# Splitting, merging and thinning the transfers of an RMS norm on one core

## The chip, the cores and the metric

The kernel runs on one NeuronCore of a Trainium2 chip. The metric is the device time in microseconds (us), as the median of several runs. Times of the kernel before and of the changed kernel are compared only between runs on the same chip, taken in turn, and all of them were at a granted clock of 1.0. DVE is the profile's name for the vector engine, ACT for ScalarE, POOL for GpSimd.

## The reference

```python
x: (16, 1024, 512) float32, gamma: (512,) float32
rms = np.sqrt(np.mean(x ** 2, axis=-1, keepdims=True) + 1e-5)
return (x / rms * gamma).astype(np.float32)
```

That is 16,384 rows of 512 floats: 33.5 MB in and 33.5 MB out, with little arithmetic on each element.

## The kernel before

The rows are cut into four tiles of 128 partitions x 32 rows (8.4 MB each), held in three buffers; tile 3 takes the buffer of tile 0. One sequencer issues every transfer, in program order.

```python
def load(t, slot, r0, r1):
    dma = nc.sync.dma_start(out=slots[slot][:, r0:r1], in_=xv[t][:, r0:r1])
    ...
def store(t, slot, r0, r1):
    dma = nc.sync.dma_start(out=ov[t][:, r0:r1], in_=slots[slot][:, r0:r1])
    ...
load(0, 0, 0, 8)
for c0, c1 in zip(pieces, pieces[1:]):          # gamma in five pieces
    nc.sync.dma_start(out=gamma_row[:, c0:c1], in_=gamma.unsqueeze(0)[:, c0:c1])
load(0, 0, 8, 16)
load(0, 0, 16, 32)
load(1, 1, 0, 32)
```

The rows of a partition lie next to each other in memory, so a transfer of n rows makes one packet of n x 2 KB for each partition, and on each of the 16 DMA engines it ends with a packet of 4 bytes for its semaphore. The compute goes in groups of up to 16 rows. ScalarE squares the rows of the next group and scales its share of the present one, DVE sums squares and multiplies by gamma, and GpSimd scales and multiplies the last `share` rows alone.

```python
groups = [                     # tile, first row, rows, pieces for the squares, GpSimd's share
    (0, 0, 7, (7,), 2), (0, 7, 9, (4, 5), 4), (0, 16, 16, (7, 5, 4), 7),
    (1, 0, 16, (7, 5, 4), 8), (1, 16, 16, (7, 5, 4), 8), (2, 0, 16, (7, 5, 4), 8),
    (2, 16, 16, (7, 5, 4), 7), (3, 0, 16, (7, 5, 4), 7), (3, 16, 16, (7, 5, 4), 3),
]
def transfers(t, g):           # issued after the group (t, g)
    if (t, g) == (0, 0):
        store(0, 0, 0, 1); load(2, 2, 0, 16)
        store(0, 0, 1, 2); load(2, 2, 16, 24)
        store(0, 0, 2, 3); load(2, 2, 24, 32)
    elif (t, g) == (0, 16):
        store(0, 0, 3, 16); store(0, 0, 16, 32)
        load(3, 0, 0, 16); load(3, 0, 16, 32)
    elif (t, g) == (1, 16): store(1, 1, 0, 32)
    elif (t, g) == (2, 0):  store(2, 2, 0, 16)
    elif (t, g) == (2, 16): store(2, 2, 16, 32)
    ...                        # tile 3 in two halves
```

(Lines are joined here to save space.)

## Time and profile before

| | before |
|---|---|
| time, median of three runs | 161.52 us (161.43 to 161.56) |
| span in the profile | 159.6 us |
| busy: DVE, ScalarE, GpSimd | 70%, 68%, 68% |
| DMA queue: data moved, share of 16 engines | 67.1 MB, 98.2% |
| last compute instruction ends | 142.2 us |
| last data packet ends | 158.4 us |

A profile like this is read from its end; the prediction below does it, with the lines. A line in the order of issues holds the start, the time that the issues took up to the end of the last, the queue (SPq is the sequencer of SyncE) and what it moved. A line of the stretches view holds the stretch, its length, busy time and count of PE, its weight loads, DVE, ScalarE and GpSimd, the clock, the DMA share, and GB/s.

### The profile page before, as it was taken

To read this page: it belongs to the slowest core of one execution; us is meant where nothing else is said; L and a number is where in the kernel's file an instruction comes from. 1 tells how busy PE (TensorE), PEld (TensorE's weight loads), DVE (VectorE), ACT (ScalarE), POOL (GpSimd) and SP (SyncE) were. 2 spreads that over 40 slices of the span, in tenths; PEclk is the share of its full clock that TensorE was granted. 3 is DMA by queue.
4 is the path that set the end of the run, shared out by engine and by line. 5 is a ranking of instruction groups with operands and counts; after the bars stand their busy time and mean duration, and the time that the engine had idled before them with its cause. 6 is when DMAs were issued, how large, how long until landed. Compare 5 with 4: busy or idle time off the path is not lost.

```text
span 159.6 us, 280 instructions
## 1 busy us (share of the span) xinstructions
PE 2.0 (1%) x2; PEld 0.5 (0%) x2; DVE 111.8 (70%) x43; ACT 108.5 (68%) x110; POOL 108.2 (68%) x24
## 2 busy tenths in 40 slices
PE   0050000000000000000000000000000000000000
PEld 0010000000000000000000000000000000000000
DVE  0027298998069899999999999999999809700000
ACT  3072999960499997989989989999995198000000
POOL 1000731981999309999999999999999999960000
DMA  5999999969799999999999999996999999999995
GB/s 199 419 435 485 435 394 526 526 263 526 329 394 396 454 415 419 427 452 444 476 394 402 509 402 394 526 526 263 526 394 394 394 501 419 394 452 468 394 419 238
DMA packets 2747, 67.12 MB, mean 421 GB/s; under 512 B 313, under 2 KB 314, under 8 KB 698
## 3 DMA queue, kind: packets, MB, share of 16 engines
q1 hardware_dynamic: 2746, 67.11, 98.2%
q14 instruction: 1, 0.01, 0.0%
HBM read 33.56 MB, written 33.55 MB: 421 GB/s over the span
## 4 chain that ended last, share of the span: by engine, by line
POOL 49%; DMA 26%; ACT 8%; DVE 3%; POOLq 2%; issue 0%
POOL slot L103 26%; DMA slot<-in_x_dram 26%; POOL slot L102 23%; ACT slot L111 3%; DVE slot L115 3%; ACT sq_psum L89 3%; POOLq L205 2%; ACT sq_sbuf L89 1%; DVE ss L96 0%; POOLq L102 0%
## 5 line engine op out<-in xcount | busy, mean ns | idle before, releaser
L102 POOL TENSOR_TENSOR slot<-slot,ss 128x3584 f32<-128x3584 f32 (+4 forms) x9 | 47.8, 5310 | 32.7 <-DVE ss L96 32.7
L90 DVE TENSOR_REDUCE ss<-sq_psum 128x7 f32<-128x3584 f32 (+1 forms) x16 | 49.1, 3066 | 20.1 <-ACT sq_psum L89 20.1
L103 POOL TENSOR_TENSOR slot<-slot,gamma_b 128x3584 f32<-128x3584 f32 (+4 forms) x9 | 60.2, 6692 | 0.7
L111 ACT ACTIVATE slot<-slot,ss 128x512 f32<-128x512 f32 x74 | 46.8, 707 | 4.7 <-DVE ss L96 4.7
L89 ACT ACTIVATE sq_psum<-slot 128x3584 f32<-128x3584 f32 (+1 forms) x16 | 40.2, 2510 | 12.4 <-DMA slot<-in_x_dram 11.0
L115 DVE TENSOR_TENSOR slot<-slot,gamma_psum 128x4608 f32<-128x4608 f32 (+4 forms) x10 | 40.8, 4093 | 4.9 <-ACT slot L111 4.9
L90 DVE TENSOR_REDUCE ss<-sq_sbuf 128x5 f32<-128x2560 f32 x8 | 22.4, 2805 | 0.0
L89 ACT ACTIVATE sq_sbuf<-slot 128x2560 f32<-128x2560 f32 x8 | 18.6, 2323 | 0.0
L95 ACT ACTIVATE ss<-ss,eps_t 128x16 f32<-128x16 f32 (+2 forms) x9 | 2.7, 303 | 4.2 <-DVE ss L90 4.2
L95 ACT ACT_TABLE_LOAD x1 | 1.3, 1283 | 4.0 <-DVE ss L90 4.0
L96 DVE RECIPROCAL ss<-ss 128x16 f32<-128x16 f32 (+2 forms) x9 | 2.1, 235 | 1.7 <-ACT ss L95 1.7
L65 PE MATMUL gamma_psum<-gamma_row,ones_col 1*128 1x512 f32 x2 | 2.0, 1118 | 8.7 <-DMA gamma_row<-in_gamma_dram 8.7
L89 ACT ACT_TABLE_LOAD x1 | 1.3, 1283 | 1.1 <-PEq L194 1.1
L160 ACT COPY gamma_b<-gamma_psum 128x512 f32<-128x512 f32 x1 | 0.6, 566 | 0.0
L65 PEld LDWEIGHTS gamma_psum<-gamma_row,ones_col 1*128 1x128 f32 x2 | 0.5, 308 | 8.7 <-issue 8.7
L63 POOL MEMSET ones_col<- 1x128 f32 x1 | 0.2, 194 | 0.3 <-POOLq L194 0.3
L194 POOL MEMSET const-float32-0.0<- 128x1 f32 x1 | 0.1, 98 | 0.2 <-issue 0.2
L194 POOL MEMSET const-bfloat16-1.0<- 128x1 bf16 x1 | 0.1, 101 | 0.0
L194 POOL MEMSET const-uint8-127<- 128x1 uint8 x1 | 0.1, 101 | 0.0
L194 POOL MEMSET const-float32-1.0<- 128x1 f32 x1 | 0.1, 98 | 0.0
L69 POOL MEMSET eps_t<- 128x1 f32 x1 | 0.1, 88 | 0.0
## 6 DMA issues: line engine op xcount, KB each, us to landing
out_dram<-slot SPq DMA_DIRECT2D x5, 4096.0 KB, 16.6
slot<-in_x_dram SPq DMA_DIRECT2D x4, 4096.0 KB, 19.3
slot<-in_x_dram SPq DMA_DIRECT2D x4, 2048.0 KB, 9.9
out_dram<-slot SPq DMA_DIRECT2D x1, 3328.0 KB, 32.4
out_dram<-slot SPq DMA_DIRECT2D x3, 256.0 KB
gamma_row<-in_gamma_dram SPq DMA_DIRECT2D x4, 0.4 KB
gamma_row<-in_gamma_dram SPq DMA_DIRECT2D x1, 0.5 KB
slot<-in_x_dram SPq DMA_DIRECT2D x1, 34.3
```

The source lines that it names most:

```text
L65: nc.tensor.matmul(gamma_psum[:, 0], ones_col, gamma_row, start=True, stop=True)
L89: nc.scalar.activation(out=sq[:, :m], in_=rows, func=AF.Square)
L90: nc.vector.tensor_reduce(out=ss[:, r : r + m, 0], in_=sq[:, :m], axis=mybir.AxisListType.X, op=OP.add)
L95: nc.scalar.activation(out=ss[:, :n, 0], in_=ss[:, :n, 0], func=AF.Sqrt, bias=eps_t, scale=1.0 / D)
L96: nc.vector.reciprocal(out=ss[:, :n, 0], in_=ss[:, :n, 0])
L102: nc.gpsimd.tensor_tensor(out=part, in0=part, in1=by_row, op=OP.mult)
L103: last = nc.gpsimd.tensor_tensor(out=part, in0=part, in1=gamma_b.to_broadcast([P, share, D]), op=OP.mult)
L111: nc.scalar.activation(out=x[:, g + r, :], in_=x[:, g + r, :], func=AF.Copy, scale=rstd[:, r])
L115: scaled = nc.vector.tensor_tensor(out=part, in0=part, in1=gamma_psum.to_broadcast([P, r1 - r0, D]), op=OP.mult)
L160: nc.scalar.copy(out=gamma_b[:, 0], in_=gamma_psum[:, 0])
L194: nc = _bacc.Bacc("TRN2", target_bir_lowering=False, num_devices=1)
L205: with _tile.TileContext(nc) as tc:
```

## The change

It rearranges transfers. Tile 1 comes in two halves, so that its first half can be squared 10 us sooner. Tile 2 is loaded and stored in one piece each. Of the three early single-row stores only the first stays. Gamma comes in one piece. GpSimd's shares are evened out, the square root's table is loaded at the start, and the last product of DVE is no longer split. GpSimd's shares and the last edit are given in words; `...` marks a cut.

```diff
-    for c0, c1 in zip(pieces, pieces[1:]):
-        nc.sync.dma_start(out=gamma_row[:, c0:c1], in_=gamma.unsqueeze(0)[:, c0:c1])
+    nc.sync.dma_start(out=gamma_row, in_=gamma.unsqueeze(0))
     load(0, 0, 8, 16)
     load(0, 0, 16, 32)
-    load(1, 1, 0, 32)
+    load(1, 1, 0, 16)
+    load(1, 1, 16, 32)
...
+    table = const.tile([P, 1], fp32)
+    nc.scalar.activation(out=table, in_=eps_t, func=AF.Sqrt)
...           (GpSimd's shares: 2, 4, 7, 8, 8, 8, 7, 7, 3 become 3, 5, 7, 7, 7, 7, 7, 7, 3)
             store(0, 0, 0, 1)
-            load(2, 2, 0, 16)
-            store(0, 0, 1, 2)
-            load(2, 2, 16, 24)
-            store(0, 0, 2, 3)
-            load(2, 2, 24, 32)
+            load(2, 2, 0, 32)
         elif (t, g) == (0, 16):
-            store(0, 0, 3, 16)
+            store(0, 0, 1, 16)
...
-        elif (t, g) == (2, 0):
-            store(2, 2, 0, 16)
         elif (t, g) == (2, 16):
-            store(2, 2, 16, 32)
+            store(2, 2, 0, 32)
...           (one times_gamma per group, the last group's too)
```

More of the change, by code (lines that the diff above doesn't have):

```diff
@@ L52 @@
     gamma_row = const.tile([1, D], fp32)
-    pieces = (0, 128, 224, 320, 416, D)
     load(0, 0, 0, 8)
-    for c0, c1 in zip(pieces, pieces[1:]):
-        nc.sync.dma_start(out=gamma_row[:, c0:c1], in_=gamma.unsqueeze(0)[:, c0:c1])
+    nc.sync.dma_start(out=gamma_row, in_=gamma.unsqueeze(0))
     load(0, 0, 8, 16)
     load(0, 0, 16, 32)
-    load(1, 1, 0, 32)
+    load(1, 1, 0, 16)
+    load(1, 1, 16, 32)
     ones_col = const.tile([1, P], fp32)
@@ L69 @@
     nc.gpsimd.memset(eps_t, eps)
+    table = const.tile([P, 1], fp32)
+    nc.scalar.activation(out=table, in_=eps_t, func=AF.Sqrt)
     groups = [
-        (0, 0, 7, (7,), 2),
-        (0, 7, 9, (4, 5), 4),
+        (0, 0, 7, (7,), 3),
+        (0, 7, 9, (4, 5), 5),
         (0, 16, 16, (7, 5, 4), 7),
-        (1, 0, 16, (7, 5, 4), 8),
-        (1, 16, 16, (7, 5, 4), 8),
-        (2, 0, 16, (7, 5, 4), 8),
+        (1, 0, 16, (7, 5, 4), 7),
+        (1, 16, 16, (7, 5, 4), 7),
+        (2, 0, 16, (7, 5, 4), 7),
         (2, 16, 16, (7, 5, 4), 7),
@@ L170 @@
         scale(rstd, t, g, 0, half)
-        if not ahead:
-            times_gamma(t, g, 0, half)
         for piece in todo[2:]:
@@ L175 @@
         scale(rstd, t, g, half, mine)
-        times_gamma(t, g, 0 if ahead else half, mine)
+        times_gamma(t, g, 0, mine)
         transfers(t, g)
```

## The prediction

> **What bounds the kernel now.** I read the page first, then the chain that ended last, then the DMA queue's own waits, then the stretches table, and last the order of the issues. The page has this on engines and queue:
>
> ```profile
> PE 2.0 (1%) x2; PEld 0.5 (0%) x2; DVE 111.8 (70%) x43; ACT 108.5 (68%) x110; POOL 108.2 (68%) x24
> ...
> DMA  5999999969799999999999999996999999999995
> ...
> DMA packets 2747, 67.12 MB, mean 421 GB/s; under 512 B 313, under 2 KB 314, under 8 KB 698
> ...
> q1 hardware_dynamic: 2746, 67.11, 98.2%
> ```
>
> No compute engine is busy above 70% of the span, while packets of the one DMA queue fill 98.2% of the time of 16 engines. A few slices show 6 or 7. I distrust those, because a packet of 64 KB is counted in the slice where it starts. The chain that ended last seems to contradict the DMA reading:
>
> ```profile
> POOL 49%; DMA 26%; ACT 8%; DVE 3%; POOLq 2%; issue 0%
> ```
>
> ```profile
> 128.16 7.79 POOL slot L103
> 135.96 2.70 POOL slot L102
> 138.66 0.04 issue
> 138.70 3.45 POOLq L205
> ```
>
> But that chain stops at 142.15 us of a span of 159.6. The 17 us after it hold no compute at all. What ends them is in the waits of the issuing sequencer (us in total, times, longest):
>
> ```profile
> SPq L49 <- DVE slot L115: 52.2, 7, 20.5
> SPq L49 <- POOL slot L103: 36.0, 5, 9.2
> SPq L45 <- DMA out_dram<-slot: 20.8, 2, 11.1
> ...
> SPq L205 <- DMA out_dram<-slot: 16.0, 2, 9.6
> ```
>
> The sequencer ends by waiting 16.0 us for the last two stores. So the end is a store's landing, not GpSimd. The long waits above it are waits before an issue; they matter only if the engines run dry meanwhile. The stretches table (the last two columns are DMA share and GB/s) says that they don't:
>
> ```profile
> 12.00:41.50 29.50, 0.00 (x0) 0.00 (x0) 22.93 (x11) 19.82 (x20) 14.56 (x5) 1.00 1.00 427
> 41.50:63.00 21.50, 0.00 (x0) 0.00 (x0) 16.92 (x6) 20.68 (x19) 14.54 (x3) 1.00 1.02 430
> ...
> 121.50:140.00 18.50, 0.00 (x0) 0.00 (x0) 12.59 (x5) 8.38 (x14) 18.34 (x5) 1.00 1.01 438
> ...
> 158.40:159.60 1.20, 0.00 (x0) 0.00 (x0) 0.00 (x0) 0.00 (x0) 0.00 (x0) 1.00 0.00 0
> ```
>
> The share is 1.0 in each of the first three, also where the compute waits for data, and in the last 1.2 us nothing moves. In the trace's packet records the first packet starts at 1.75 us and the last ends at 158.41 us, and in every 1 us bin between them 16 packets are in flight on average, to within one. The kernel is one unbroken stream of 156.7 us, plus 1.75 us ahead and 1.2 us behind. The reported time is 161.52 - 159.6 = 1.9 us more than the span. A change helps only by shortening the stream, and hurts only by making it longer or putting a hole in it.
>
> **What the Trainium skill says.** "DMA: Bandwidth & Descriptors", section "Where 436 GB/s comes from", gives 435.2 GB/s as the ceiling of the SBUF ports and about 358 as the HBM share of a core. The trace agrees with the first: 67.11 MB in 156.66 us are 428 GB/s. It does not show the 358 with this core alone. The same page, section "Anatomy of one DMA — SWDGE (gpsimd) path", says that DMA engines do not wait on semaphores; the issuing sequencer waits, and the engines drain their queues. The trace agrees: the sequencer waits tens of us and the stream has no hole. Its section "Bandwidth" (Measured) advises at least 1 MiB per DMA. That was measured on single transfers; the 256 KB row stores here queue behind other work, so I size their cost from the packets instead. "ScalarE: Activation LUTs", section "What ACT_TABLE_LOAD costs", has about 1283 ns for a table load; the two loads here took 1283 ns each.
>
> **The change part by part.** A 128-partition transfer gives each of 16 engines 8 packets, one per partition. Median packet times in the records are 0.084 us for 2 KB, 0.611 for 16 KB, 0.987 for 26 KB, 1.213 for 32 KB and 2.418 for 64 KB. A straight line fits all of them: 9 ns per packet plus bytes at 27.2 GB/s. A semaphore packet of 4 bytes took 9 ns too. The bytes don't change, so the stream changes by 9 ns for every packet per engine.
>
> Before: 9 loads of x and 10 stores, 19 x 8 = 152 data packets per engine (2,432 / 16 in the records), and 19 semaphore packets. After: 8 loads (three of tile 0, two of tile 1, one of tile 2, two of tile 3) and 7 stores (row 0 of tile 0, rows 1 to 15, rows 16 to 31, tile 1, tile 2, two halves of tile 3). That is 15 x 8 = 120 data packets and 15 semaphore packets.
>
> - Second tile in two halves: 8 more packets, +0.072 us.
> - Third tile loaded whole instead of in three: 16 fewer, -0.144. Stored whole instead of in two: 8 fewer, -0.072.
> - Two single-row stores folded into the larger store: 16 fewer, -0.144.
> - Four fewer semaphore packets: -0.036.
> - Sum: -0.324 us on the stream.
> - Gamma: five packets of 22 to 27 ns become one of 2 KB on one engine. This saves at most 8 x 9 = 0.07 us on that engine alone; I count none of it. It also frees the sequencer: five issues take 1.60 us from 1.17, one takes about 0.36. The second load can be issued some 1.2 us earlier, but the first one keeps the engines busy until 7 us.
> - Table load: a dummy square root is put ahead. After the second table load of the kernel before, Square and Copy ran with no third, so one set serves all three. The 1.28 us load at 15.09 should go. It is off the stream: 0.
> - Shares: three groups go from 8 to 7 GpSimd rows, so GpSimd takes 6.16 + 7.77 = 13.93 us instead of 7.02 + 8.88 = 15.9 in each. With the first half of tile 1 landing near 32 us, ScalarE need not sit idle from 36.67 to 42.23. The compute gains about 5.6 us there and 3 x 2 on GpSimd, some 12 us by the end. It all lies beside the stream: 0.
> - DVE's last product is no longer split: 13 rows after all scaling, about 7 us instead of the last 3.9. That spends 3 of the 12 us.
>
> 161.52 - 0.32 = 161.20 us.
>
> **The rivals.** First, a hole from the later store of tile 2. It now waits for the whole tile. The issues before stand at:
>
> ```profile
> 92.12 50.39 SPq L49 DMA_DIRECT2D out_dram<-slot  x5
> ```
>
> ```profile
> 60.01 0.34 SPq L49 DMA_DIRECT2D out_dram<-slot  x1
> 71.62 10.43 SPq L45 DMA_DIRECT2D slot<-in_x_dram  x2
> ```
>
> The five are tile 1 at 92.12, the halves of tile 2 at 108.0 and 122.0, and those of tile 3 at about 136 and 142.2. The queue needs tile 2 at about 119, when the packets of tile 1's store end. At the old pace, the whole store at 122.0 would come 3 us late. By my count GpSimd starts (1,0) at about 54.3, when its factors can be ready, instead of 60.2, and finishes (2,16) four groups of 13.93 later, at 110. That leaves 9 us. If the compute gains nothing, the hole costs 3 us and the time is about 164.5. I think this unlikely, because ScalarE's idle 5.56 us before the tile was put down to its landing.
>
> Second, the compute becomes faster and the kernel with it, as the chain of waits suggests (GpSimd 49%): ending 12 us earlier would give about 150. Against it: 428 GB/s without a hole. I give it almost nothing.
>
> Third, the order of transfers itself. The packets took 1.1 us per engine more than their medians: about 0.5 us in the first microseconds of the stream, 0.37 around 38 us in the last packets of tile 1's load, 0.14 around 62 us, where loads give way to stores. Why, the profile doesn't say. With other sizes at these places this may shrink or grow by 0.3 us. It would make 160.9 to 161.5.
>
> Fourth, the single load of tile 2 behind the row store: if it were issued after 41.5 us, the engines would run dry. The row store went out at 27.13 before, and its rows are ready at about the same time after, since the table load that goes saves what the two additional rows on ScalarE and DVE cost. Slack 14 us.
>
> **Range and chances.** The sum is small and sure in sign; the irregular 1.1 us is what can blur it, and the three runs before lie within 0.13 us. Predicted 161.2 us, 8 in 10 between 160.8 and 161.6. More than 2% faster would be under 158.3; 67.12 MB over 16 engines at 27.2 GB/s each are 154.2 us of pure bytes, and with 1.75, 1.2 and 1.9 us around them 159.1 at best, so 0.5%. More than 2% slower, over 164.8, needs the first rival in full and more: 1.5%. Within 2%: 98%.
>
> **What would show it right or wrong.** Right: DMA share 1.0 from 1.75 to about 158.1 us; 15 issues of x and out; 2,163 packets for 2,747 (512 of data, 64 of semaphores and 8 of gamma fewer); one table load; last compute some 4 to 12 us earlier than 142 with no gain from it; a longer final wait of the sequencer for stores; tile 2's store issued before 119. Wrong: a stretch near 42, 62, 81 or 119 us with a DMA share well below 1, or packets of one size that took other times than these medians.

## The result, and the profile after

| | before | changed |
|---|---|---|
| time, median of four runs each, same chip | 161.54 us (161.43 to 161.66) | 161.63 us (161.56 to 161.99) |
| span in the profile | 159.6 us | 159.5 us |
| DMA packets | 2747 | 2163 |
| last compute ends | 142.2 us | 137.9 us |
| last data packet ends | 158.41 us | 158.35 us |

The ratio is 1.001, with a 95% interval of 0.9992 to 1.0027. A ratio is the mean time of one kernel's fast runs over that of the other's fast runs of the same rounds, so it is not quite the ratio of the two medians. The time is the same, as forecast. But the 0.32 us that the prediction put down as a gain are not there, and the median lies 0.03 us above its range.

The page of the changed kernel has the same picture as before:

```profile
PE 2.0 (1%) x2; PEld 0.5 (0%) x2; DVE 112.6 (71%) x42; ACT 108.1 (68%) x111; POOL 106.4 (67%) x24
...
DMA packets 2163, 67.12 MB, mean 421 GB/s; under 512 B 241, under 2 KB 241, under 8 KB 370
...
q1 hardware_dynamic: 2162, 67.11, 98.2%
```

584 packets went, exactly as counted ahead, and yet the share of the span and the mean rate did not move. The sequencer's own waits of the changed kernel:

```profile
SPq L45 <- DMA out_dram<-slot: 28.0, 2, 18.3
SPq L197 <- DMA out_dram<-slot: 20.2, 3, 9.6
```

The final wait for stores (the second line) grew from 16.0 to 20.2 us: the compute ended 4.3 us sooner, and all of that became waiting. GpSimd's last instruction ended 12.8 us sooner, at 129.3 instead of 142.2 us, but DVE's last product, no longer split, now waits for all 13 rows of ScalarE and ends last:

```profile
130.83 7.09 DVE L115 TENSOR_TENSOR slot<-slot,gamma_psum 128x6656 f32<-128x6656 f32 x1 [8.13 <-ACT slot L111]
```

The stretches view of the changed kernel, for the same stretches:

```profile
12.00:41.50 29.50, 0.00 (x0) 0.00 (x0) 24.91 (x12) 23.77 (x21) 20.39 (x5) 1.00 1.00 425
41.50:63.00 21.50, 0.00 (x0) 0.00 (x0) 20.84 (x9) 20.07 (x24) 19.62 (x4) 1.00 1.02 432
...
121.50:140.00 18.50, 0.00 (x0) 0.00 (x0) 8.28 (x3) 8.07 (x13) 7.75 (x3) 1.00 1.02 441
```

In the first stretch ScalarE is busy for 23.8 us instead of 19.8 and GpSimd for 20.4 instead of 14.6: the half tile is used as soon as it lands. In the third they have less left to do. (Part of GpSimd's growth is its larger shares in tile 0.) The DMA columns are as before. And the store of tile 2, in the order of issues:

```profile
109.17 0.34 SPq L49 DMA_DIRECT2D out_dram<-slot  x1
```

It went out 10 us before the queue came to it, at about 119.4. The prediction had 110. The table load is gone too; the first line is of the kernel before, the second of the changed one, both ScalarE in order of time:

```profile
15.09 1.28 ACT L95 ACT_TABLE_LOAD   x1 [4.01 <-DVE ss L90]
```

```profile
15.03 0.30 ACT L95 ACTIVATE ss<-ss,eps_t 128x7 f32<-128x7 f32 x1 [3.96 <-DVE ss L90]
```

So the unbroken stream, the issues in time, the packet count and the table load came as told. The gain did not, and for that one has to go below the views, to the packet records.

**How the stream is measured here.** The trace has a record of start, duration and size for each packet. A transfer's length in the table below is the mean end of its last 16 packets (one for each engine) less the same for the transfer ahead of it; for the first load it is counted from the mean start of the first 16 packets. These lengths are also compared between the batches of experiments, which ran on four chips: most transfers repeat within a few ns in all profiles. An undisturbed 8.4 MB transfer in 64 KB packets takes 19.32 us, and two of half the size in 32 KB packets take 9.68 each.

| transfer, us | before | changed |
|---|---|---|
| first load (16 KB packets) | 5.41 | 5.43 |
| tile 1's load | 19.72 | 9.68 + 10.05 |
| row 0's store | 0.73 | 0.72 |
| tile 2's load with the row stores inside it | 20.76 | 19.60 |
| store of the rest of the half tile | 7.87 | 9.08 |
| tile 2's store | 9.68 + 9.68 | 19.32 |
| mean end of the stream | 158.16 | 158.11 |

Two things stick out. Tile 2's load and the rows that moved out of it fell by 1.16 us, but the store that took the rows in grew by 1.21. And 9.68 against 10.05: the second half of tile 1 has the same bytes as the first and took 0.37 us more. In both kernels, loads that are followed by the first stores end with slow packets. The places near 42 and 62 us where the queue goes over from loads to stores are called turns below. The experiments ask how much a packet costs in the stream, and what the slow packets are.

### The profile page after: what moved, and what is told of

It is laid out like the page before. It is cut to its first block, busy times and chain, and to the rows that moved or that the text cites. A ratio compares the mean times of both kernels' runs of the same rounds, so it can differ in the third digit from the quotient of the medians.

```text
span 159.5 us, 266 instructions
## 1 busy us (share of the span) xinstructions
PE 2.0 (1%) x2; PEld 0.5 (0%) x2; DVE 112.6 (71%) x42; ACT 108.1 (68%) x111; POOL 106.4 (67%) x24
## 2 busy tenths in 40 slices
DMA packets 2163, 67.12 MB, mean 421 GB/s; under 512 B 241, under 2 KB 241, under 8 KB 370
## 4 chain that ended last, share of the span: by engine, by line
DMA 38%; DVE 29%; ACT 16%; issue 2%; ACTq 0%; SPq 0%
DMA out_dram<-slot 22%; DMA slot<-in_x_dram 17%; DVE ss L90 17%; DVE slot L115 12%; ACT slot L111 8%; ACT sq_psum L89 6%; ACT sq_sbuf L89 1%; ACTq L197 0%; ACT ss L95 0%; ACT gamma_b L154 0%; DVE ss L96 0%; SPq L49 0%; ACTq L89 0%
## 5 line engine op out<-in xcount | busy, mean ns | idle before, releaser
L102 POOL TENSOR_TENSOR slot<-slot,ss 128x3584 f32<-128x3584 f32 (+2 forms) x9 | 46.9, 5216 | 21.7 <-DVE ss L96 21.7
L103 POOL TENSOR_TENSOR slot<-slot,gamma_b 128x3584 f32<-128x3584 f32 (+2 forms) x9 | 59.2, 6582 | 0.7
L111 ACT ACTIVATE slot<-slot,ss 128x512 f32<-128x512 f32 x75 | 47.4, 707 | 4.7 <-DVE ss L96 4.7
L115 DVE TENSOR_TENSOR slot<-slot,gamma_psum 128x4608 f32<-128x4608 f32 (+2 forms) x9 | 41.3, 4593 | 8.5 <-ACT slot L111 8.5
```

The costliest lines, as they stand in the source:

```text
L102: nc.gpsimd.tensor_tensor(out=part, in0=part, in1=by_row, op=OP.mult)
L103: last = nc.gpsimd.tensor_tensor(out=part, in0=part, in1=gamma_b.to_broadcast([P, share, D]), op=OP.mult)
L111: nc.scalar.activation(out=x[:, g + r, :], in_=x[:, g + r, :], func=AF.Copy, scale=rstd[:, r])
L115: scaled = nc.vector.tensor_tensor(out=part, in0=part, in1=gamma_psum.to_broadcast([P, r1 - r0, D]), op=OP.mult)
```

## The experiments

Fourteen kernels ran (two of them without an edit), in four batches, each with fresh runs of the kernel before on the same chip. All gave the right result. Medians of the kernel before in these batches were 161.65 to 161.78 us, but single runs of it went up to 164.13. In the last batch two of 11, at 164.05 and 164.13, are slow and left out of its ratios, though their granted clock was 1.0.

**The kernel before and the changed kernel again** (no edit).

> The kernel before, unchanged, timed against itself: it shows the noise that any difference of 0.1 to 0.3 us has to be seen against. Both theories: ratio 1.000 with an interval of about 0.1%, time 161.4 to 161.7. Its second profile tells whether the slow last packets of a load ahead of a store (0.35 us per engine near 42 us, 0.14 near 62 us in the first profile) come back at the same places. Theory 'place': same places, within 0.05 us. Rival 'chance': other places or other sizes by 0.2 us.

> The changed kernel again, on the same chip as the kernel before. Theory 'place' (the change keeps its 0.31 us of saved packet time but pays about 0.2 us back in slower last packets near 62 us, always): ratio 0.999 to 1.000, the profile again with some 0.35 us near 42 and near 62 us. Rival 'chance' (the pay-back was bad luck of the runs): ratio 0.998, time near 161.2 as predicted.

Measured: 161.60 us (161.41 to 161.74) and 161.62 us (161.55 to 161.73), six runs each. Their ratios to the runs of the kernel before are 0.9982 (0.994 to 1.0024) and 0.9986 (0.9948 to 1.0024). The ratio of the kernel before to itself lies as far from 1 as the changed kernel's, mostly because one of the 11 shared runs was at 163.74. So the gain of 0.2% that 'chance' asked for is not there: the medians differ by 0.02 us. The slow packets came back at the same places: over their undisturbed length, the loads ahead of the two turns took 0.26 and 0.37 us more in the kernel before (0.40 and 0.14 the first time), and 0.32 and 0.36 in the changed kernel (0.37 and 0.37). So the places are fixed, as 'place' said, but the sizes scatter by 0.2 us, as 'chance' said.

**What does a packet cost?** The same store in 2 KB packets.

```diff
-            store(2, 2, 0, 32)
+            for odd in (0, 1):      # every second row: 2 KB packets
+                dma = nc.sync.dma_start(out=ov[2][:, odd:R:2], in_=slots[2][:, odd:R:2])
+                before_scale.append((2, 0, 32, dma))
```

> The changed kernel with tile 2 stored as its even and its odd rows, two transfers of 2 KB packets instead of one of 64 KB packets: 512 packets per 2 engines' worth of partitions, that is 256 per engine instead of 8, the same bytes. Theory 'each packet costs 9 ns of the stream': 248 x 0.009 = 2.23 us longer than the changed kernel, about 163.9 us, all of it in the stretch of that store. Rival 'packet overhead is hidden by pipelining, so the packet count of my prediction was worth nothing': no change, 161.6 us.

Measured: 163.17 us (163.05 to 163.5) beside 161.62 for the changed kernel in the same rounds, so +1.55 us. Its page, and the stretch of that store, first of this kernel, then of the changed one:

```profile
DMA packets 6147, 67.12 MB, mean 416 GB/s; under 512 B 257, under 2 KB 257, under 8 KB 4482
```

```profile
119.00:140.00 21.00, 0.00 (x0) 0.00 (x0) 10.99 (x3) 8.07 (x13) 10.45 (x3) 1.00 1.01 394
```

```profile
119.00:140.00 21.00, 0.00 (x0) 0.00 (x0) 10.78 (x3) 8.07 (x13) 10.25 (x3) 1.00 1.01 438
```

The share is 1.01 in both, yet the rate fell from 438 to 394 GB/s: a full queue is not a fast one, and only the last column shows it. From the start of tile 1's store to the end the stream took 59.43 us instead of 58.01. That is 1.42 us for 248 packets and one more semaphore, 5.7 ns each. The records of the 2 KB packets say 84 ns as before, 9 ns more than their bytes, but they come 80 to 81 ns apart on an engine: the records overlap. Neither theory had it. The packets count, but at 5.7 ns and not at 9. One thing this edit does not keep apart: the store's packets also go to every second row, so their addresses change along with their size. The two halves of tile 2's store, with neighbouring rows, give 4.9 ns (see below).

**Does the time hang on the compute?** Two steps back. First tile 1 whole again:

```diff
-    load(1, 1, 0, 16)
-    load(1, 1, 16, 32)
+    load(1, 1, 0, 32)
```

> The changed kernel with one part undone: tile 1 loaded whole again. Theory 'the stream sets the time': tile 2's store is then issued at about 116 us, still before the queue needs it at 119.4, so no hole; 8 packets x 5 to 6 ns less, 0.05 us: 161.6 us within the noise of 0.1. Rival 'the compute or the earlier half tile matters': the (1,0) squares start 7 us later and the time rises by some of it, 162.5 us or more.

Measured: 161.61 us (161.47 to 161.83), beside 161.68 for the kernel before. The store of tile 2 went out 7.4 us later, and no hole came of it:

```profile
116.58 0.34 SPq L49 DMA_DIRECT2D out_dram<-slot  x1
```

Then GpSimd's old shares on top of this edit.

> The changed kernel with tile 1 loaded whole and the shares of GpSimd of the kernel before, so the compute runs as late as before while tile 2 is stored whole. Theory of the prediction's first rival (a hole before tile 2's store): the store is issued at 122.0 instead of 109, the queue has run dry at 119.4, the first packet follows about 1 us after the issue: a hole of 3 to 3.7 us, time 164.6 to 165.3 us, DMA share well below 1 between 119 and 123. Rival 'slack elsewhere covers it': 161.6 us.

Measured: 164.80 us (164.80 to 165.00), ratio 1.0185 (1.0155 to 1.0215): slower, but by a little less or a little more than 2%. The issue, and the stretches about it (packets are booked where they start, so the 1049 is 16 packets of 64 KB):

```profile
121.93 0.34 SPq L49 DMA_DIRECT2D out_dram<-slot  x1
```

```profile
119.00:120.00 1.00, 0.00 (x0) 0.00 (x0) 1.00 (x2) 1.00 (x3) 1.00 (x1) 1.00 0.01 0
120.00:121.00 1.00, 0.00 (x0) 0.00 (x0) 1.00 (x1) 1.00 (x3) 1.00 (x1) 1.00 0.00 0
121.00:122.00 1.00, 0.00 (x0) 0.00 (x0) 1.00 (x2) 0.45 (x2) 1.00 (x2) 1.00 0.00 0
122.00:123.00 1.00, 0.00 (x0) 0.00 (x0) 1.00 (x1) 0.18 (x1) 1.00 (x1) 1.00 2.46 1049
```

This is the hole of the prediction's first rival: the queue ran dry near 119.4, and the first packet started at 122.77 us, 0.84 us after the issue. Tile 2's store took 22.80 us instead of 19.32, and 3.2 of these 3.5 us are in the time (164.80 beside 161.61). After the hole the slowest engine ends only 0.1 us behind the mean, where it was 0.25 us behind without the hole. So the split of tile 1 and the new shares together pay for storing tile 2 whole. Without the split alone, the issue came 2.7 us before the first engine ran out, of which 0.84 us pass before packets start, so some 2 us of slack were left; the old shares alone were not tried. Without both the change costs 1.9%.

**What are the slow packets?** The changed kernel without the early row store:

```diff
+    load(2, 2, 0, 32)               # right after tile 1
 ...
-            store(0, 0, 0, 1)
-            load(2, 2, 0, 32)
 ...
-            store(0, 0, 1, 16)
+            store(0, 0, 0, 16)
```

> The changed kernel without the early single-row store: row 0 goes out with rows 1 to 15, and tile 2's load follows tile 1's with no store between. Theory 'switch' (last packets of a load are slowed where the queue turns from loads to stores): one turn less, so no slow packets near 42 us, 0.33 us saved there, and 8 + 1 packets x 9 ns = 0.08 us, together 0.4 us under the changed kernel, 161.2 us. Rival 'chance or the first store of all': the slow packets only move to the first store near 61 us and grow there, saving 0.08 us, 161.5 us.

Measured: 161.97 us (161.82 to 163.02). With no store near 42 us, tile 1's second half took 9.68 us, undisturbed. But tile 2's load took 20.32 instead of 19.32: all of the cost, 1.0 us, came at the first store near 61 us. Nothing was saved by one turn less, so the 'switch' theory fell, and the rival was right about where the slow packets go, though not about the time (161.5 us told).

Then two parts of the change alone, on the kernel before. First the rows folded into the larger store, then tile 2's load whole with the three row stores in a row ahead of it:

```diff
-            store(0, 0, 1, 2)       # e2: both row stores go, and store(0, 0, 3, 16)
-            store(0, 0, 2, 3)       #     becomes store(0, 0, 1, 16)
```

```diff
+            store(0, 0, 1, 2)       # e3: three rows, then the load in one piece
+            store(0, 0, 2, 3)
+            load(2, 2, 0, 32)
```

> The kernel before with only the second and third single-row store folded into the larger store; tile 2 still loaded in three pieces. Read from the packets: from the end of row 0's store to the end of the store of the rest of the half tile took 28.63 and 28.86 us in two profiles of the kernel before. Theory 'packets cost 9 ns each': 0.16 us less. Theory 'packet records overlap, 5 to 6 ns, and the next load already starts inside a row store': 0.08 us less. On slow packets at the turn near 62 us: 'size of the last load's packets' keeps 0.13 to 0.36 us as before; 'length of the unbroken load' gives 0.35 or more, as in the changed kernel. Time 161.5 to 161.6 us.

> The kernel before with only tile 2's load whole, the three single-row stores together ahead of it. Theory 'size of the last load's packets or length of the unbroken load': 0.35 us of slow packets at the turn near 62 us, as in the changed kernel, against 0.13 to 0.36 before. The load itself in 64 KB packets: 19.24 us without the turn (19.32 less 0.08 that lies inside the row stores). Rival 'the folded rows carry the slow turn': 0.13 to 0.2 us at the turn. Time 161.5 to 161.6 us.

Measured: 162.09 us (161.82 to 162.41) and 162.21 us (162.15 to 162.26), beside 161.68; ratios 1.0015 (0.9982 to 1.0048) and 1.0022 (0.9992 to 1.0051), so not told from 1. With the rows folded, the path from row 0's store to the end of the larger store took 28.78 us, within the 28.63 and 28.86 of the kernel before. But the slow packets near 62 us were 0.35 us of it, against 0.14 and 0.37. Less these, the path is 28.43 us, against 28.49 in both profiles of the kernel before: 0.07 us saved, close to the 0.08 of the second theory and not to 0.16. (The time shows nothing of it; this profile lost 0.3 us near 99 us.) The other run bears on the slow packets: with three rows stored at the first turn, tile 1's load took 20.27 instead of 19.32 us, 0.95 more, and near 62 us there was no loss at all (19.21 us for tile 2's load). What was paid at the first turn was not paid at the second. None of the expectations had this.

Four more kernels from the changed one:

```diff
-            load(2, 2, 0, 32)       # e1
+            load(2, 2, 0, 16)
+            load(2, 2, 16, 32)
```

> The changed kernel with tile 2 loaded as two transfers in a row, 32 KB packets instead of 64 KB, no store between them. What makes the last packets of a load slow where the queue turns to stores? So far, added over the turns near 42 and near 62 us: 0.5 and 0.6 us in two profiles of the kernel before, 0.67 to 0.93 in four of the changed one and its variants, 0.94 with three rows stored at once at the first turn (all of it there, nothing at the second), 1.0 with no row store (all at the second). Theory 'packet size': the turn near 62 us falls from 0.35 to below 0.2. Rival 'a debt of the start, paid at the first stores, whatever the packets': 0.3 to 0.5 near 62 us, 0.65 to 0.95 in all. Plus 0.044 us for eight packets. Time 161.6 to 161.8 us.

Measured: 161.77 us (161.60 to 162.21) beside 161.78. Near 62 us only 0.06 us, but near 42 us 0.56. The packet size theory was right for its turn, but what was missing there was paid at the other: the sum, 0.62 us, lies in the range of the other profiles. The rival had the sum nearly right (0.65 or more told) and the turn near 62 us wrong. It is one profile, and the sizes scatter.

```diff
-    load(1, 1, 16, 32)               # e4
 ...
             store(0, 0, 0, 1)
+            load(1, 1, 16, 32)
```

> The changed kernel with the single-row store between the two halves of tile 1, so that the first turn comes at 31.6 instead of 41.6 us. Theory 'debt of unbroken loading': first turn 0.25 us or less, the second, after 30 us of loads, larger than 0.35. Rival 'cost of the first stores, whenever they come': 0.3 to 0.4 at the first and 0.3 to 0.5 at the second, as in the changed kernel.

Measured: one run, 163.84 us. Slow packets cost 0.22 us at 31 us and 0.59 us near 60 us, on the mean of the engines. That fits the theory of a debt of loading, but also the scatter. The profile also shows one way in which a run can be 2 us longer: one engine was 1.3 us behind most of the others at 58 us, its last packet ahead of the turn then took 3.95 us instead of 2.42, and at the end it was alone at work from 158.5 to 160.7 us. Sixteen engines have equal shares, so the time is the slowest one's.

```diff
-            store(0, 0, 1, 16)       # e5: and tile 3's halves in the other order
             store(0, 0, 16, 32)
+            store(0, 0, 1, 16)
```

> The changed kernel with the second half of tile 0 stored ahead of rows 1 to 15 at the turn near 62 us, and tile 3's halves loaded in the other order to fit; the end is not of interest here, a small hole there is possible. Theory 'the addresses written at the turn matter' (rows 0 and 1 to 15 share a region, rows 16 to 31 are further off): the turn near 62 us is below 0.15 or above 0.6 us. Rival 'they don't': 0.3 to 0.5 us as in the changed kernel.

Measured: one run, 161.98 us. 0.24 us near 42 us and 0.64 near 62. By its letter (above 0.6) that is for the theory of addresses, by the size of the scatter it is nothing. Inconclusive. The small hole came: tile 2's store was issued at 118.92 us, its first packet started 0.84 us later, and the store took 0.23 us more than the 19.32 without a hole.

```diff
     load(0, 0, 8, 16)
+    store(0, 0, 0, 3)                # e6: unscaled rows, overwritten later
```

> The changed kernel with three unscaled rows of tile 0 stored as early as they have landed, turning the queue to a store at 12 us; they are overwritten later with the right result, so the output stays correct. The extra 786 KB cost 1.85 us of stream. Theory 'cost of the first stores, whenever they come': 0.5 us or more at the turn at 12 us and less than 0.2 us in all at the turns near 44 and 64 us. Rival 'debt of unbroken loading': less than 0.25 us at 12 us and still 0.5 us or more at the two later turns.

Measured: one run, 164.38 us, right result. The load ahead of the early store took 6.09 us instead of 4.87: 1.22 us at 12 us. After that, no loss at either turn: 9.68 us for tile 1's second half and 19.25 for tile 2's load. The loads had run for only 10 us by then, so no debt of long loading can be meant. In these profiles the cost goes with the first stores of the execution, whether they came at 12, 42 or 61 us, and is not paid again after them.

**With that cost out of the way.** The same early store in both kernels:

> The kernel before with the three unscaled rows stored early as well, so that the one-time cost of the first stores is paid at 12 us in both kernels and the turns near 44 and 64 us carry none. Theory 'packets alone separate the two kernels, at 5 to 6 ns, and the first-store cost is only scatter on top': without the scatter, from the end of tile 1's load to the end of tile 3's second store, 0.15 to 0.2 us more than the changed kernel with the same early store. Rival 'the prediction's 9 ns a packet': 0.32 us more. Time about 164.4 us like the changed kernel's, with 0.3 us of noise.

> The changed kernel with the same early store, a second time and timed. Both theories: turns near 44 and 64 us with less than 0.1 us of slow packets; the cost at 12 us again 0.5 to 1.3 us. The stream from the end of tile 1's load to the end 116.2 to 116.3 us as in its first profile; 0.15 to 0.2 us shorter than the kernel before's if packets cost 5 to 6 ns, 0.32 if 9.

Measured: 164.62 us (164.55 to 164.84) for the kernel before with the early store, 164.52 us (164.40 to 164.80) for the changed one. From the end of tile 1's load to the end of the stream the first took 116.44 us and the second 116.22 (116.23 in the profile of e6): 0.21 to 0.23 us less, a little over the 0.15 to 0.2 expected and well under 0.32. Tile 1's load, 19.32 whole and 19.36 in halves, takes 0.04 of it back. So the packets of the whole change are worth 0.17 to 0.19 us, about 5 ns for each of the 36, and not 0.32. The cost of the first stores was 1.40 and 1.35 us here.

## Why the prediction was right or wrong

Right: the bound. The stream of packets sets the time, it has no hole in the changed kernel, and compute that ends 4.3 us sooner is worth nothing. Tile 2's store was issued at 109.2 (110 told), and by the way told: GpSimd started the first group of tile 1 at 53.1 (54.3 told). The row store went out 16 us ahead of need (14 told), one table load is left, and 2,163 packets are recorded, as told. The first rival, the hole, was priced well: 3 us and 164.5 us told, a hole of 3.5 us and 164.8 us measured once both of the parts that keep it away were taken out. "Same" was right.

Wrong: the sum, "-0.324 us on the stream". The step that failed is its factor: "the stream changes by 9 ns for every packet per engine". It took the length of a packet's record for the time that the packet adds to the stream. Records overlap at their ends; packets came 5.7 ns apart beyond their bytes (2 KB packets) and 4.9 ns (8 packets and a semaphore, 19.367 less 19.323 us for tile 2's store). The count of 36 was right; 36 x 5.7 = 0.21 us, or 36 x 4.9 = 0.18, was the sum to make. The pair with the early store gave 0.17 to 0.19. The term that was furthest off is the folded rows: a row store alone takes 0.72 us in the sequence, but the load after it is 0.08 us shorter than its bytes ask, so 0.64 us was to be saved for a row and 0.60 us was paid for it in the larger store. Two folded rows were worth 0.08 us, not 0.16 (0.144 and two semaphore packets). The prediction's own signs of being wrong could not catch this: the median records of 16, 32 and 64 KB packets are the same in the changed kernel (0.611, 1.213 and 2.418 us), and the share stayed at 1. Both are read from records, and records do not show how closely packets follow each other. ("To within one" is also not quite so: in the bin from 2 to 3 us 14.3 packets are in flight.)

Mis-sized beside the stream: the compute. GpSimd ended 12.8 us sooner ("some 12" told), but the unsplit product spent 8.6 of that and not 3: it took the 7 us told, but could not start before ScalarE's rows, at 130.83 us. It cost nothing here.

Mis-sized as well: the noise. The prediction named the slow packets as its third rival, and said that they may change by 0.3 us, but then drew a range of 0.4 us to either side of a time that left them as they were. In the two profiles of the kernel before they cost 0.54 and 0.63 us, in the two of the changed one 0.74 and 0.68. That alone takes back 0.13 us of the 0.17 to 0.19 on the mean, and 0.20 in the first pair of profiles, where the stream ended only 0.05 us sooner. What is left is as small as the 0.05 us between two medians of the kernel before on one chip (161.60 and 161.65); that the changed kernel's median came out 0.09 us higher is not told from chance.

Open: whether the changed kernel's larger cost of the first stores is its own or scatter. Over the variants with turns near 42 and 62 us it was 0.65 (rows folded) and 0.93 (three rows first) from the kernel before, and 0.62, 0.79, 0.84, 0.88 and 0.94 from the changed one. The two sets overlap. What causes it was not found; shown is only that it goes with the first stores and is not paid again after them. No variant was faster than either kernel by more than the noise.

## What to carry to other kernels

When the queue is full from end to end, only bytes, packets and holes count: ask of each rearranged transfer whether it is issued before the queue runs dry (here the first packet came 0.84 us after the issue), and what its packets cost. Take a packet's cost from how far apart packets follow each other, not from the length of their records; a share of 1.0 says that the engines are occupied, not that they move much. And a gain of 0.2% is not to be promised where the kernel against itself differs by as much.

## What the Trainium skill lacked or had wrong

- "DMA: Bandwidth & Descriptors", section "Bandwidth", gives about 10.5 ns for a packet as the floor of a 4 KB transfer that GpSimd issues, and elsewhere counts the overhead of a packet in cycles. It has no measured time for what one packet more costs in a queue that a sequencer keeps full. Here that was 5.7 ns beyond its bytes for 2 KB packets, and 0.04 us for cutting one transfer in two (8 packets and a semaphore more on each engine, 4.9 ns each).
- No page has the extra cost of the first stores of an execution. It shows as slow last packets of the loads ahead of them: 0.54 to 1.40 us on the mean of the 16 engines in the profiles here, and up to 1.5 us more on a single engine.
- "DMA: Bandwidth & Descriptors", section "Where 436 GB/s comes from", says that for transfers between HBM and SBUF the HBM share of about 358 GB/s binds. The stream of this kernel, on one core, ran at 428 GB/s. The page's section "Bandwidth" fits that (425 GB/s for one core alone, about 358 for each of two that stream together), so it is the sentence that lacks its condition.
